# Hybrid Hyena and attention backbone: the front of layer 0 ordered by channel halves, its filter butterflies on VectorE

## The chip, the cores and the metric

The kernel runs on one core of a Trainium2 chip. The metric is the device time in microseconds (us) of one execution; the time before is the median of three runs. TensorE, VectorE, ScalarE and GpSimd are named PE, DVE, ACT and POOL in the profile; PEld is TensorE's loading of weights, SP the engine that only issues DMAs.

## The reference

A trunk of two layers over 1024 tokens of width 1024, with 256 context tokens, all in float32. Layer 0 joins two mixers. The Hyena mixer projects 3 x 512 channels (v, x1, x2), puts a short convolution of three taps over each, and then twice convolves over the whole sequence with a filter that a small network makes:

```python
def hyena_mix(proj, conv_w, conv_b, w1, b1, freq, w2, b2, w3, d_skip):
    proj = dwconv3(proj, conv_w, conv_b)
    v, x1, x2 = jnp.split(proj, 3, axis=-1)
    filt = hyena_filters(L, w1, b1, freq, w2, b2, w3)
    z = v
    for o, gate in enumerate((x1, x2)):
        z = gate * fftconv_bidir(z, filt[:, o], d_skip[o])
    return z
```

The other is differential attention of four heads, whose keys and values come from the tokens and from the context, with rotary positions on q and k. Both go through one output projection. Behind them stand a convolutional feed-forward network, layer 1 (a spatial gating unit) and a second feed-forward network; none of these is touched.

## The kernel before

The change lies in `layer0_front`, the first quarter of the kernel. Matrices are split into a high and a low part (`split`, L144): the high part is a cast on ScalarE, the low part a subtraction on VectorE or GpSimd, and a product is three matmuls (`mm3`, L156). The strings at the top, such as `F_PART` and `F_H`, say with a letter for each operation whether VectorE (V) or GpSimd (G) does it.

The front first makes the normalised input: `hhi[k]`, `hlo[k]` (eight tiles of 128 channels by 1024 tokens, L409 to 417; `F_H` chooses the engine of the low parts) and `hch`, `hcl` for the context. Then two generators run:

- `main` (L785) is the projections, TensorE's work: `proj_v` (values of tokens and context), `proj_kc` (keys of the context), `proj_hyena` (12 units of 128 channels: for each half of the 512 Hyena channels the kinds v, x1, x2, each in two units; a unit is 96 matmuls and two shifted multiply-adds on VectorE, L672 to 674), and `proj_qk` (8 units; each is rotated with a table `tab`, L756, and stored).
- `side` (L789) is the long convolutions. `filters` (L505) makes the spectra of all filters and stores them to `Hd` in DRAM: for each of two orders it loads and splits w3 (1024 columns), and for each half of the channels and each side `sd` it makes one set: products with the window (`z`), and `dft_part` (L470), a transform whose first step is matmuls and whose second is 13 small sums, the butterflies, which `F_PART` places. Then `conv_chain` (L614) for each half: transform of `z`, product with the stored spectrum, inverse transform, gate, twice over. It stops where `z`, x1 or x2 of its half is not yet projected.

`eager` (L161) traces the two: the side as far as it goes, then one step of main, and so on. So all eight sets of filters are traced first, then proj_v, proj_kc and the first three Hyena units, then the first part of the convolution chain, and so on. The traced order is not yet the engines' order. A planner at compile time gives each engine its list: among the instructions whose operands and buffers it reckons to be ready, the one traced earlier goes first, and what stands under `first()` (L185) counts as traced 4000 instructions earlier. The lists are fixed; at run time each engine and each DMA queue works in its own order and waits on semaphores.

Buffers come from pools and are given in the planner's order. `f8` (L306, 7 tiles of 128x2048 float32) holds `hch`, `hcl`, the raw and split w3, `z` of each half and the operands of all transforms, and the table `tab`; attention loads its first head into the same seven. `t4` (4 tiles of 128x1024) serves the projections and the last step of the chain. `h8` (2 tiles) holds the window, the spectra and the gates. In `proj_qk` the two parts of the rotated result go to `t4`, or to `h8` when the side has been traced to its end (L766). Weights come by SP's queue into two buffers, and w3 (L512), `dskip` (L526) and the table by the same queue; stores and `h8` loads go by ScalarE's queue.

```python
            def main():
                for gen in (proj_v(), proj_kc(), proj_hyena(), proj_qk()):
                    yield from gen

            def side():
                yield from filters()
                ld(tbi, ap["dfti"])
                for half in range(2):
                    yield from conv_chain(half)
                done.add("side")
```

Of the kernel before, what the change touches and what calls it, by code (L numbers as in the profile page):

```python
# [92 lines left out]
def tile_kernel(ctx: ExitStack, tc: tile.TileContext, ap: dict, out: bass.AP, stop=None):  # L93
# [6 lines left out]
    def nm(s):  # L100
        uid[0] += 1
        return f"{s}_{uid[0]}"
# [185 lines left out]
    def layer0_front(fp):  # L288
        with ExitStack() as es:
# [10 lines left out]
            def ps4():  # L300
                return ps2("pf").rearrange("p (r n) -> p r n", r=4)
# [4 lines left out]
            def f8(dt=F32):  # L306
                return fp.tile([P, 2, 4, CH], dt, tag="f8", name=nm("f8"))

            def f8z(dt=F32):
                return f8(dt).rearrange("p a b n -> p (a b) n")  # L310

            def h8(src, shape):
                t = h8pool.tile([P, 2048], F32, tag="h8", name=nm("h8"))
                st(t, src)
                return t.rearrange("p (a b c) -> p a b c", a=shape[0], b=shape[1])
# [186 lines left out]
                stt(V, X[:, 1, 2:4], u[:, 1, 0:2], -RT2, t[:, 1, 0:2], MUL, ADD)  # L502
                return X

            def filters():  # L505
                h2r = h2s.rearrange("p (s r) -> p r s", r=8)
                for o in range(2):
                    raw = f8()
                    w3, w3s = raw.rearrange("p a b n -> p a (b n)")[:64, 0], None
                    w3 = raw[:64, 0].rearrange("p (a b) n -> p a (b n)", a=2)  # L510
                    w3s = raw[:64, 1].rearrange("p (a b) n -> p a (b n)", a=2)
# [3 lines left out]
                    ws = f8(F32R)  # L515
                    w3h = ws[:, 0].rearrange("p (a b) n -> p a (b n)", a=2)
                    w3l = ws[:, 1].rearrange("p (a b) n -> p a (b n)", a=2)
                    A.copy(out=w3h[0:64], in_=w3s)
                    A.copy(out=w3h[64:128], in_=w3s)
                    sub(V, w3l[0:64], w3s, w3h[0:64])  # L520
                    sub(V, w3l[64:128], w3s, w3h[0:64])
                    for half in range(2):
                        win = h8(ap["window"][half], (1, 8))[:, 0]
                        cs = slice(half * CH, (half + 1) * CH)
                        dsk = tp.tile([P, CH], F32, tag="dsk", name=nm("dsk"), bufs=1)
                        ld(dsk[0:1], ap["dskip"][o : o + 1, cs])  # L526
                        for sd in range(2):
                            z = f8z()
                            for g in range(2):
                                ps = ps4()  # L530
                                for r in range(4):
                                    mm(ps[:, r], h2r[:, g * 4 + r], w3h[:, sd, cs], True, False)
                                    mm(ps[:, r], h2r[:, g * 4 + r], w3l[:, sd, cs], False, True)
                                gs = slice(g * 4, g * 4 + 4)
                                mul(V, z[:, gs], ps, win[:, gs])
                            if sd == 0:

                                p0 = ps2("pf")
                                mm(p0[:, :CH], h2r[:, 0], w3h[:, 1, cs], True, False)
                                mm(p0[:, :CH], h2r[:, 0], w3l[:, 1, cs], False, True)  # L540
                                f0 = tp.tile([P, CH], F32, tag="f0", name=nm("f0"), bufs=1)
                                mul(V, f0[0:1], p0[0:1, :CH], win[0:1, 0])
                                add(V, f0[0:1], f0[0:1], z[0:1, 0])
                                V.tensor_scalar(out=f0[0:1], in0=f0[0:1], scalar1=0.5, scalar2=None, op0=MUL)
                                stt(V, z[0:1, 0], dsk[0:1], 1.0 / S, f0[0:1], MUL, ADD)
                            yield
                            X = yield from dft_part(z, sd, 2 * o + half)
                            for par in range(2):
                                st(Hd[o, half, par][:, sd * 1024 : (sd + 1) * 1024],
                                   X[:, par].rearrange("p a b -> p (a b)"))  # L550
                            yield


            zs, done = {}, set()
# [163 lines left out]
                        st(Kd[h, i][:, S:], r32(t[:, i * CTX : (i + 1) * CTX]))  # L718
                    yield

            def proj_hyena():
                z = {}

                def post(half, kind, j, a):
                    if kind == 2:
                        st(x2d[2 * half + j], a)
                        done.add((1, half, j))
                        return
                    ps = to_time(a)
                    if kind == 0:  # L730
                        if j == 0:
                            z[half] = f8z()
                        with first():
                            A.copy(out=z[half][:, :, j * P : (j + 1) * P], in_=ps)
                        if j == 1:
                            zs[half] = z[half]
                    else:
                        t = t4()
                        with first():
                            A.copy(out=t, in_=ps.rearrange("p r c -> p (r c)"))  # L740
                        st(x1d[half][:, :, j * P : (j + 1) * P], t.rearrange("p (r c) -> p r c", r=8))
                        done.add((0, half, j))

                pend = None
                for half in range(2):
                    for kind in range(3):
                        for j in range(2):
                            a = conv_mtile(4 * kind + 2 * half + j)
                            if pend:
                                post(*pend)  # L750
                            pend = (half, kind, j, a)
                            yield
                post(*pend)

            def proj_qk():
# [39 lines left out]

# [1078 lines left out]
```

## Time and profile before

| | |
|---|---|
| time, median of 3 runs | 2723.33 us (2721.12 to 2727.28) |
| the profiled execution: its time | 2731.36 us |
| the profiled execution: its span | 2729.3 us |
| busy, share of the span | PE 91%, DVE 66%, ACT 44%, POOL 40% |
| mean granted clock of TensorE | 0.959 |
| instructions | 30518 |

The span is the time from the first to the last instruction of the profiled execution; the time of that execution is 2 us longer. The shares are means over stages with different limits, so a change in one stage has to be read from that stage.

### The profile page before, as it was taken

To read this page: it belongs to the slowest core of one execution; us is meant where nothing else is said; L and a number is where in the kernel's file an instruction comes from. 1 tells how busy PE (TensorE), PEld (TensorE's weight loads), DVE (VectorE), ACT (ScalarE), POOL (GpSimd) and SP (SyncE) were. 2 spreads that over 40 slices of the span, in tenths; PEclk is the share of its full clock that TensorE was granted. 3 is DMA by queue.
4 is the path that set the end of the run, shared out by engine and by line. 5 is a ranking of instruction groups with operands and counts; after the bars stand their busy time and mean duration, and the time that the engine had idled before them with its cause. 6 is when DMAs were issued, how large, how long until landed. Compare 5 with 4: busy or idle time off the path is not lost. (4 is left out here: it accounts for less than half of the span.)

```text
span 2729.3 us, 30518 instructions
## 1 busy us (share of the span) xinstructions
PE 2482.1 (91%) x11192; PEld 1978.6 (72%) x11192; DVE 1795.3 (66%) x2119; ACT 1205.1 (44%) x1871; POOL 1086.2 (40%) x819
## 2 busy tenths in 40 slices
PE   6799878697888899999999899999999999999897
PEld 1798767576777667777777777778877777777676
DVE  4677788878896485666666966532366665567854
ACT  2312211026665256555554355313356566555342
POOL 1323111103443352423334777413343433438775
PEclk8899998898999899999999999999999999999998
DMA  7224222257732446988787634111436777769422
GB/s 284 66 101 166 85 101 85 70 186 231 201 100 66 162 116 152 246 218 228 201 224 254 227 115 147 39 45 48 156 84 148 179 167 171 180 155 320 143 81 101
DMA packets 166854, 412.75 MB, mean 151 GB/s; under 512 B 16011, under 2 KB 28815, under 8 KB 164528
## 3 DMA queue, kind: packets, MB, share of 16 engines
q1 hardware_dynamic: 86352, 248.76, 28.7%
q0 software_dynamic: 34848, 63.45, 13.6%
q10 hardware_dynamic: 45504, 98.58, 9.8%
q8 instruction: 88, 1.44, 0.2%
q14 instruction: 62, 0.51, 0.1%
HBM read 261.31 MB, written 85.98 MB: 127 GB/s over the span
## 5 line engine op out<-in xcount | busy, mean ns | idle before, releaser
L154 PE MATMUL b<-u,u 128*128 128x512 f32 (+1 forms) x5624 | 1328.5, 395 | 66.3 <-POOL u L132 25.6
L154 PEld LDWEIGHTS b<-u,u 128*128 128x128 f32 x5624 | 1060.2, 191 | 332.9 <-POOL u L132 36.5
L132 DVE TENSOR_TENSOR u<-u,u 128x512 fp32r<-128x512 f32 (+2 forms) x470 | 468.5, 1024 | 334.8 <-ACT u L1141 173.9
L132 POOL TENSOR_TENSOR u<-u,u 128x512 fp32r<-128x512 f32 (+1 forms) x338 | 505.4, 1516 | 295.5 <-ACT u L1141 176.6
L1152 POOL DMA_DIRECT2D u<-u x242 | 211.3, 920 | 490.3 <-ACT u L1151 378.4
L1141 ACT CAST u<-u 128x512 fp32r<-128x512 f32 x462 | 261.6, 616 | 231.4 <-DVE u L132 96.8
L154 PE MATMUL b<-x,u 128*128 128x512 f32 x1224 | 296.8, 397 | 1.8 <-ACT u L1342 1.1
L128 DVE SCALAR_TENSOR_TENSOR u<-u,cols,u 128x1023 f32<-128x1023 f32 x176 | 232.6, 1328 | 95.2 <-ACT u L1588 87.1
L154 PEld LDWEIGHTS b<-x,u 128*128 128x128 f32 x1224 | 229.4, 188 | 62.9 <-issue 3.4
L1150 ACT CAST u<-u 128x512 fp32r<-128x512 f32 x242 | 146.2, 614 | 120.8 <-DVE u L132 94.7
L132 POOL TENSOR_TENSOR wlo<-wraw,whi 128x1024 fp32r<-128x1024 f32 x24 | 68.9, 2874 | 314.2 <-ACT whi L147 311.1
L1151 ACT ACTIVATE u<-u 128x512 fp32r<-128x512 f32 x242 | 149.4, 628 | 71.8 <-POOL u L132 62.7
L132 DVE TENSOR_TENSOR u<-u,b 128x512 f32<-128x512 f32 (+1 forms) x132 | 112.1, 860 | 66.0 <-PE b L154 65.2
L132 DVE TENSOR_TENSOR f<-f 128x256 f32<-128x256 f32 (+3 forms) x232 | 148.4, 699 | 1.0
L154 PE MATMUL pj<-hh,whi 128*128 128x512 f32 x320 | 130.7, 408 | 19.8 <-ACT t L740 8.3
L1588 ACT ACTIVATE u<-u,cols 128x1024 f32<-128x1024 f32 x88 | 109.3, 1242 | 87.5 <-DVE u L132 85.0
L128 DVE SCALAR_TENSOR_TENSOR x<-b,mods,x 128x512 f32<-128x512 f32 (+1 forms) x104 | 88.7, 906 | 66.4 <-PE b L154 66.4
L154 PE MATMUL pj<-hl,whi 128*128 128x512 f32 x320 | 128.0, 400 | 0.0
L154 PE MATMUL pj<-hh,wlo 128*128 128x512 f32 x320 | 127.9, 400 | 0.0
L132 POOL TENSOR_TENSOR p<-p,p 128x1280 f32<-128x1280 f32 x27 | 79.6, 2948 | 121.2 <-ACT p L885 103.3
L874 ACT ACTIVATE p<-s,nx 128x1280 f32<-128x1280 f32 x64 | 84.9, 1328 | 44.7 <-DVE nx L870 41.8
L147 ACT CAST whi<-wraw 128x1024 fp32r<-128x1024 f32 x28 | 29.2, 1047 | 164.2 <-PE pj L154 145.8
(225 smaller groups left out, 3115.8 us busy)
## 6 DMA issues: line engine op xcount, KB each, us to landing
u<-u POOLq DMA_DIRECT2D x242, 256.0 KB, 4.6
u<-wup SPq DMA_DIRECT2D x88, 512.0 KB, 4.7
Td<-u ACTq DMA_DIRECT2D x66, 512.0 KB, 5.6
u<-Td SPq DMA_DIRECT2D x56, 512.0 KB, 4.4
wraw<-modw SPq DMA_DIRECT2D x48, 512.0 KB, 5.3
u<-wdown SPq DMA_DIRECT2D x40, 512.0 KB, 5.8
wraw<-modw0b SPq DMA_DIRECT2D x32, 512.0 KB, 3.9
xs<-x ACTq DMA_DIRECT2D x48, 256.0 KB, 2.1
```

The costliest lines, as they stand in the source:

```text
L128: eng.scalar_tensor_tensor(out=o, in0=a, scalar=sc, in1=b, op0=op0, op1=op1)
L132: eng.tensor_tensor(out=o, in0=a, in1=b, op=op)
L147: A.copy(out=hi, in_=x)
L154: T.matmul(o, l, r, start=st and not onto, stop=sp, skip_group_check=onto)
L874: A.activation(q.p[m], q.s, AF.Exp, bias=q.nx, accum_out=q.l[:, m : m + 1])
L1141: A.copy(out=t[:, H0], in_=x)
L1150: A.copy(out=t[:, H0], in_=x)
L1151: A.activation(t[:, H1], t[:, H0].bitcast(F32), AF.Copy, scale=-1.0)
L1152: G.dma_start(out=t[:, H1], in_=x, accum_op=ADD)
L1588: A.activation(a, c, AF.Identity, bias=col(f"fb{l}", f), scale=col(f"fw{l}1", f))
```

## The change

Filters and projections are ordered by channel halves. `filters` takes a half and makes the four sets of that half only (both orders, both sides); its w3 load and split take 256 of 512 columns of each side and happen four times instead of twice. `proj_hyena` takes a half too. `main` runs Hyena's first half, the values, Hyena's second half, the context keys, then queries and keys. `side` runs filters and convolution of half 0, then filters and convolution of half 1. All letters of `F_PART` and `F_H` become V.

```diff
-F_PART = ("VGGGVGGVVVVVG", "VGGVVGGVVVVVV", "VGGGVGGVVVVVG", "VGGVVGGVVVVVV", "VGGGVGGVVVVVG", "VGGVVGGVVVVVV", "VGGGVGGVVVVVG", "VGGVVGGVVVVVV")
+F_PART = ("V" * 13,) * 8
...
-F_H, F_X, F_SQ = "VGVVGVVG", "VVVVVVVV", ("V", "V", "V", "V", "V", "V", "V")
+F_H, F_X, F_SQ = "VVVVVVVV", "VVVVVVVV", ("V", "V", "V", "V", "V", "V", "V")
...
-            def filters():
+            def filters(half):
                 h2r = h2s.rearrange("p (s r) -> p r s", r=8)
+                cs = slice(half * CH, (half + 1) * CH)
                 for o in range(2):
...
+                    raw, ws = f8(), f8(F32R)
+                    w3, w3s = (raw[:64, i, 0:2] for i in range(2))
-                    ld(w3, ap["hy_w3"][:, o])
+                    ld(w3, ap["hy_w3"][:, o, :, cs])
                     add(V, w3s[:, 0], w3[:, 0], w3[:, 1])
                     sub(V, w3s[:, 1], w3[:, 0], w3[:, 1])
...
-                    for half in range(2):
-                        win = h8(ap["window"][half], (1, 8))[:, 0]
-                        cs = slice(half * CH, (half + 1) * CH)
+                    win = h8(ap["window"][half], (1, 8))[:, 0]
...
-            def proj_hyena():
+            def proj_hyena(half):
                 z = {}
...
-                for half in range(2):
-                    for kind in range(3):
-                        for j in range(2):
-                            a = conv_mtile(4 * kind + 2 * half + j)
+                for kind in range(3):
+                    for j in range(2):
+                        a = conv_mtile(4 * kind + 2 * half + j)
...
             def main():
-                for gen in (proj_v(), proj_kc(), proj_hyena(), proj_qk()):
+                for gen in (proj_hyena(0), proj_v(), proj_hyena(1), proj_kc(), proj_qk()):
                     yield from gen
 
             def side():
-                yield from filters()
                 ld(tbi, ap["dfti"])
                 for half in range(2):
+                    yield from filters(half)
                     yield from conv_chain(half)
                 done.add("side")
```

## Rows read from the trace of the kernel before

**Rows 1.** The page's second part: TensorE's busy tenths in 40 slices.
```profile
PE   6799878697888899999999899999999999999897
```

**Rows 2.** Timeline of TensorE: start us, duration us, instruction, [idle before <-releaser].
```profile
546.70 9.46 PE L154 MATMUL pf<-tbi,f 128*128 128x128 f32 x64 [25.11 <-DVE f L132]
...
619.04 2.43 PE L154 MATMUL s<-f,f 128*128 128x512 f32 x6 [2.53 <-ACT t L773]
```

**Rows 3.** By stretch: busy us (xcount) of PE, PEld, DVE, ACT, POOL; clock; DMA.
```profile
76.00:111.00 35.00, 25.26 (x145) 23.80 (x145) 23.26 (x17) 15.80 (x20) 15.64 (x5) 0.70 0.16 50
111.00:191.00 80.00, 78.56 (x483) 74.43 (x482) 56.63 (x77) 14.97 (x16) 21.22 (x22) 1.00 0.33 114
191.00:270.00 79.00, 74.96 (x394) 66.78 (x394) 59.67 (x79) 17.27 (x21) 30.71 (x26) 1.00 0.42 142
270.00:296.00 26.00, 21.87 (x98) 18.08 (x97) 6.30 (x6) 7.12 (x7) 4.70 (x2) 0.93 0.19 61
296.00:430.00 134.00, 105.49 (x483) 88.39 (x482) 116.31 (x145) 20.68 (x20) 20.33 (x6) 0.90 0.27 94
430.00:565.00 135.00, 102.15 (x471) 85.03 (x471) 119.07 (x149) 17.52 (x17) 13.93 (x4) 0.89 0.29 91
```

**Rows 4.** Timeline of all engines around 270 to 299 us.
```profile
269.28 0.68 DVE L128 SCALAR_TENSOR_TENSOR f<-f,f 128x512 f32<-128x512 f32 x1
...
275.36 1.00 ACT L734 COPY f<-pj 128x1024 f32<-128x1024 f32 x1
...
291.11 1.00 ACT L734 COPY f<-pj 128x1024 f32<-128x1024 f32 x1
...
295.99 2.48 DVE L132 TENSOR_TENSOR f<-pf,f 128x1024 f32<-128x1024 f32 x2 [2.15 <-PE pf L154]
```

**Rows 5.** Timeline of ScalarE and its DMA queue over the front.
```profile
107.82 0.40 ACTq L704 DMA_DIRECT2D Vd<-t  x1
...
236.01 0.33 ACTq L718 DMA_DIRECT2D Kd<-t  x1
...
410.39 1.93 ACT L734 COPY f<-pj 128x1024 f32<-128x1024 f32 x2 [11.86 <-DVE f L132]
...
570.48 1.02 ACT L773 ACTIVATE t<-pj 128x1024 f32<-128x1024 f32 x1 [11.20 <-DMA yd<-t]
...
617.97 1.02 ACT L773 ACTIVATE t<-pj 128x1024 f32<-128x1024 f32 x1 [1.66 <-DVE h L132]
```

**Rows 6.** Waits of SP's queue, 0 to 640 us: in total, times, longest.
```profile
SPq L526 <- DVE f L128: 58.3, 3, 38.0
...
SPq L758 <- DVE f L132: 14.6, 1, 14.6
```

**Rows 7.** VectorE by shape, 296 to 565 us: busy us, mean ns.
```profile
L132 DVE TENSOR_TENSOR f<-f 128x256 f32<-128x256 f32 x92 | 38.5, 486 | 0.1
L128 DVE SCALAR_TENSOR_TENSOR t<-pj,cols,t 128x1023 f32<-128x1023 f32 x18 | 22.9, 1274 | 2.2 <-ACT t L672 2.2
```

**Rows 8.** Groups by shape in the filter stage, 111 to 270 us.
```profile
L132 DVE TENSOR_TENSOR f<-f 128x256 f32<-128x256 f32 x56 | 34.1, 646 | 0.8
...
L132 POOL TENSOR_TENSOR f<-f 128x256 f32<-128x256 f32 x40 | 32.0, 808 | 98.5 <-DVE f L132 92.8 <-PE pf L154 4.7 <-DMA Kd<-t 0.2
```

**Rows 9.** Timeline of VectorE in the filter stage.
```profile
111.64 1.22 DVE L132 TENSOR_TENSOR f<-pf,h 128x1024 f32<-128x1024 f32 x1 [8.89 <-PE pf L154]
...
184.07 0.68 DVE L132 TENSOR_TENSOR f<-f 64x512 f32<-64x512 f32 x1
...
190.69 1.23 DVE L132 TENSOR_TENSOR f<-pf,h 128x1024 f32<-128x1024 f32 x1 [2.37 <-PE pf L154]
```

**Rows 10.** DMA issues, 100 to 270 us: KB each, median us to landing.
```profile
Hd<-f ACTq DMA_DIRECT2D x16, 512.0 KB, 3.2
```

**Rows 11.** Timeline of GpSimd while h is split.
```profile
91.47 4.08 POOL L132 TENSOR_TENSOR hl<-t,hh 128x1024 fp32r<-128x1024 f32 x1 [3.61 <-ACT hh L147]
```

**Rows 12.** VectorE's groups by shape, 70 to 640 us.
```profile
L132 DVE TENSOR_TENSOR t<-t,f 128x1024 f32<-128x1024 f32 x16 | 20.8, 1340 | 0.1
```

More of the change, by code (lines that the diff above doesn't have):

```diff
@@ L503, in dft_part @@
                 return X
[L505 removed]
+            def filters(half):
                 h2r = h2s.rearrange("p (s r) -> p r s", r=8)
+                cs = slice(half * CH, (half + 1) * CH)
                 for o in range(2):
[L508 to L511, printed above, removed]
[L512 removed]
+                    raw, ws = f8(), f8(F32R)
+                    w3, w3s = (raw[:64, i, 0:2] for i in range(2))
+                    ld(w3, ap["hy_w3"][:, o, :, cs])
                     add(V, w3s[:, 0], w3[:, 0], w3[:, 1])
                     sub(V, w3s[:, 1], w3[:, 0], w3[:, 1])
[L515 to L517 removed]
+                    w3h, w3l = (ws[:, i, 0:2] for i in range(2))
                     A.copy(out=w3h[0:64], in_=w3s)
@@ L521, in filters @@
                     sub(V, w3l[64:128], w3s, w3h[0:64])
-                    for half in range(2):
-                        win = h8(ap["window"][half], (1, 8))[:, 0]
-                        cs = slice(half * CH, (half + 1) * CH)
[L525 to L551, printed above, removed]
@@ new lines, in filters @@
+                    win = h8(ap["window"][half], (1, 8))[:, 0]
+                    dsk = tp.tile([P, CH], F32, tag="dsk", name=nm("dsk"), bufs=1)
+                    ld(dsk[0:1], ap["dskip"][o : o + 1, cs])
+                    for sd in range(2):
+                        z = f8z()
+                        for g in range(2):
+                            ps = ps4()
+                            for r in range(4):
+                                mm(ps[:, r], h2r[:, g * 4 + r], w3h[:, sd], True, False)
+                                mm(ps[:, r], h2r[:, g * 4 + r], w3l[:, sd], False, True)
+                            gs = slice(g * 4, g * 4 + 4)
+                            mul(V, z[:, gs], ps, win[:, gs])
+                        if sd == 0:
+                            p0 = ps2("pf")
+                            mm(p0[:, :CH], h2r[:, 0], w3h[:, 1], True, False)
+                            mm(p0[:, :CH], h2r[:, 0], w3l[:, 1], False, True)
+                            f0 = tp.tile([P, CH], F32, tag="f0", name=nm("f0"), bufs=1)
+                            mul(V, f0[0:1], p0[0:1, :CH], win[0:1, 0])
+                            add(V, f0[0:1], f0[0:1], z[0:1, 0])
+                            V.tensor_scalar(out=f0[0:1], in0=f0[0:1], scalar1=0.5, scalar2=None, op0=MUL)
+                            stt(V, z[0:1, 0], dsk[0:1], 1.0 / S, f0[0:1], MUL, ADD)
+                        yield
+                        X = yield from dft_part(z, sd, 2 * o + half)
+                        for par in range(2):
+                            st(Hd[o, half, par][:, sd * 1024 : (sd + 1) * 1024],
+                               X[:, par].rearrange("p a b -> p (a b)"))
+                        yield
@@ L744, in proj_hyena @@
                 pend = None
-                for half in range(2):
-                    for kind in range(3):
-                        for j in range(2):
-                            a = conv_mtile(4 * kind + 2 * half + j)
[L749 to L752, printed above, removed]
+                for kind in range(3):
+                    for j in range(2):
+                        a = conv_mtile(4 * kind + 2 * half + j)
+                        if pend:
+                            post(*pend)
+                        pend = (half, kind, j, a)
+                        yield
                 post(*pend)
```

## The prediction

> **What bounds the kernel now.** I read the page's slices first, then TensorE's idle places, a table of engine time by stretch over the front, the timelines around single places, and groups by shape. Behind the front TensorE is busy in nine tenths of most slices, and the front lasts to about 619 us, when the first attention scores start [rows 1, 2]; nothing behind it is touched, so what the front gains or loses should arrive at the end one for one.
>
> The front divides at places that rows show. From 76 to 111 the normalised input is made. From 111 to 270 the eight filter sets run (two filter orders, two halves, two sides), about 19.8 us each; TensorE is nearly full here (78.6 of 80, 75.0 of 79), filled by the value and context-key projections, while VectorE works 56.6 + 59.7 = 116.3 of 159 us [rows 3]. From 270 to 296 VectorE has almost nothing, 6.3 of 26 us: the filters are done at 269.96, but the first forward transform needs the first half's projected z, whose two copies end at 276.4 and 292.1, and its first sum starts at 295.99 [rows 3, 4]. From 296 to 430 and from 430 to 565 the two convolution chains run with VectorE at 116.3 of 134 and 119.1 of 135 us: they are one serial chain of VectorE work. TensorE then lacks 28.5 and 32.9 us [rows 3]. Two causes can be seen: before 410 the copies of the second half's z wait 11.86 us for VectorE to give up a tile [rows 5], and before 546.7 TensorE stands 25.11 us behind VectorE's inverse transform [rows 2]. The load of the rope table depends on nothing but a free `f8` tile, and SP still waits 14.6 us for VectorE before it [rows 6]; the rotations of q and k start after it. Behind the chain TensorE has query/key units left, one each (617.97 - 570.48) / 5 = 9.5 us [rows 5]. So what sets the start of attention is VectorE's chain from 111 to 565, plus five query/key units.
>
> **The change part by part**, as differences on that chain.
>
> *The gap at 270.* z of half 0 is now the first thing projected. In the old order two units were 15.75 us apart [rows 4]; from about 92 us both are done near 130, long before four filter sets end. What stays is the way from a ready z to the first sum, 295.99 - 292.11 = 3.9 us. 26.0 - 3.9: -22 us. I choose this in full, since z has about 60 us to spare.
>
> *Short convolution off the chain.* Of 24 such VectorE instructions 18 lie between 296 and 565, 1.274 us each [rows 7]. Half of the 24 now fall into the first filter stage, where VectorE idles: six fewer on the busy chain, -8. Bounds -8 and 0.
>
> *Butterflies.* F_PART turns 40 GpSimd instructions (808 ns) into VectorE ones [rows 8]. At the 486 ns of the same shape in the convolution stage [rows 7] that is +19.4. Against it: in the filter stage the 56 that VectorE has already take 646 ns [rows 8]; at 486 they give back 56 x 0.16 = 9.0. VectorE is also idle 159 - 116.3 = 43 us in the eight sets, 5.3 per set [rows 3], and the five even-half operations of a set (2.4 us) need only the first pair of PSUM reads, so they can lie in such a wait. Bounds +19 (none hidden, nothing given back) and -9 (all hidden); I take +2, nearer to hidden, since the wait is longer than the work. That VectorE slows beside GpSimd is what these two means show. The Trainium skill (SBUF — State Buffer, section on the two physically separate sides) says that the two share a port pair as an exclusive lock, for which a VectorE instruction with two SBUF inputs competes, and the loser blocks for the whole instruction. By it up to 40 x 0.81 = 32 us of blocking could go, and this term would be -13 where I have +2; 160 ns more per instruction is much less than that.
>
> *Weights of the filters.* w3 is prepared four times at half size instead of twice. One cost the way from 184.07 to the next product at 190.69, 6.6 us [rows 9]; I estimate 4.5 at half width, since part of it is cast and waiting. 4 x 4.5 - 2 x 6.6 = +5. Bounds 0 and +13 (two more at full price).
>
> *Tiles.* The `f8` pool has seven. The context halves `hch`, `hcl` are read by proj_v and proj_kc, which were over at 236 [rows 5]; proj_kc is now behind both Hyena halves, so two tiles stay held far longer, and z of half 0 holds a third through the first four sets. With the filter weights that leaves three for z, a, b, t, X. It can still run (b is free before X is needed) but the next set's two products, 1.22 us each [rows 9], no longer overlap with the last sums: 3 boundaries x 2.4 = +7. Bounds 0 and +70: per set 2.4 plus X's two stores in turn, 3.2 us each to land [rows 10], 8.8 x 8.
>
> *Filling.* The second half's filters are traced behind the first chain and may run in its waits: 134 - 116.3 = 17.7 us [rows 3]. Bounds -17.7 and 0; -5, for want of tiles.
>
> *Splits of h.* Three low halves go from GpSimd, whose last took 4.08 us [rows 11], to VectorE, where 128x1024 operands take 1.22 [rows 9]: the last about 3 us earlier, -3; bounds -4 and 0.
>
> *SP's queue.* Four w3 loads instead of two and four dskip loads now stand among the Hyena weights. SP stood up to 38 us on a dskip wait [rows 6]; behind it are projection weights. Two units of weights in hand cover 19 us of TensorE, and VectorE's chain doesn't wait for them: 0, bound +19. GpSimd only loses work; it issues no loads here.
>
> *The tail.* Unit 0 of the query/key projection took its two output halves from the four `t4` tiles, since the side was not yet traced to its end; with proj_kc between, all eight use `h8`, and one more unit can stand done before the chain ends. -9.5; bounds -47.5 (all five) and +9.5.
>
> Sum: -22 - 8 + 2 + 5 + 7 - 5 - 3 - 9.5 = -33.5 us. The profiled execution has a span of 2729.3 and a time of 2731.4, 8 us above the median 2723.3; that offset is not touched, so I forecast 2723.3 - 33.5 = 2690, with 2672 to 2708 as this case's own range.
>
> **The rivals.**
> - *Tiles starve the filters; slower.* The place is the first writer of X or of the next z, the price up to 8.8 us per set. At full price +70 stands for +7: -33.5 + 63, 2753. It decides from (7 + 33.5) / 8 = 5.1 us per set. For it: the rope load, which needs only a free tile, found none until the last transform [rows 6], so the pool is always full. Against it: the old filters also ran beside `hch`, `hcl`, with only one tile more. Chance 0.17.
> - *VectorE is the bound; nothing gained.* Butterflies at +19.4, no hiding of short convolutions (0), no filling (0): -33.5 + 17.4 + 8 + 5 = -3, 2720. Against it: VectorE is idle 43 of 159 us in the filter stage [rows 3]. The Trainium skill (Perfetto Trace Analysis, Optimizing Scalar/DVE Operations) advises handing work from a saturated VectorE to others, even GpSimd; by that rule this change goes the wrong way in the convolution stage, but the moved work lies where the trace shows idle time. Chance 0.11.
> - *The rope table gets a tile early; more gained.* Four more units move before the chain's end, 4 x 9.5 = -38, but bring a shuffle, two products, a sum and a split of VectorE each, by the products' 1.34 us [rows 12] an estimated 6.5, +26: 2678. Against it: the table has the last claim on tiles. Chance 0.12. All of TensorE's idle time from 76 to 565, 9.7 + 1.4 + 4.0 + 4.1 + 28.5 + 32.9 = 80.6 us [rows 3], gives the floor, 2643.
> - *The order does not change on the engines.* They follow a compiled order, not the text: a tile of proj_v was stored at 107.82, before the first product of the filters at 111.64, which are traced ahead of it [rows 5, 9]. If the planner fills as before, only butterflies and weights change: +7 or less, 2723 to 2730. Chance 0.06.
>
> **How the numbers follow.** The forecast has 0.54. The range runs from just above the floor, 2645, to 2735, which leaves out most of the starving case (about 0.14) and a little below. A change of 0.2% (5.4 us) is about what a measurement of this kernel can tell from none. Faster: 0.54 + 0.12 + 0.04 of the VectorE case + 0.02 of a mild starving = 0.72. Same: 0.05 + 0.04 + 0.01 = 0.10. Slower: 0.02 + 0.02 + 0.14 = 0.18.
>
> **What would show it.** Right: no idle stretch of VectorE between the fourth filter set and the first forward sum; filter sets of 18 to 21 us; first scores near 585 instead of 619; four or fewer query/key units after the last inverse transform; no GpSimd work on 128x256 tiles. Wrong: VectorE waiting between sets with X's stores or tile releases as the cause (sets of 25 us or more), z of half 1 waiting tens of us for a tile with TensorE empty, or a longer row of query/key units after the chain.

## The result, and the profile after

The changed kernel takes 2686.73 us (median of 4 runs, 2685.09 to 2689.07) against 2725.28 for the kernel before (4 runs): 38.5 us less, ratio 0.9861 with a 95% interval of 0.9844 to 0.9878. The profiled spans are 2729.3 and 2686.4 us. The forecast was 2690, so the gain was 5 us larger than forecast (38.5 for 33.5). The sum was right; several of its terms were not, and their errors cancelled.

The front is shorter. Its end is taken here at the first score matmul, 615.21 before and 577.88 after: 37.3 us. The row at 619.04 [rows 2], which the prediction took for the first scores, is the second row of them. The code behind the front is not touched, but the time from the first scores to the end of the span isn't quite the same from one profiled execution to the next: 2114.1 us before, 2108.5 after, and between 2104.4 and 2115.7 in the fourteen kernels of this document. So a few us of a time need not come from the front, and 5.6 of the 42.9 us between the two spans don't. The last stand of TensorE before the inverse transform fell from 25.11 to 14.88 us. VectorE's last product of the chain and TensorE's first scores before, and the same places after:

```profile
564.34 1.20 DVE L132 TENSOR_TENSOR t<-pf,t 128x1024 f32<-128x1024 f32 x1
615.21 1.30 PE L154 MATMUL s<-f,f 128*128 128x512 f32 x6
```

```profile
513.19 3.17 PE L154 MATMUL pf<-tbi,f 128*128 128x128 f32 x13 [14.88 <-DVE f L132]
...
524.36 1.22 DVE L132 TENSOR_TENSOR t<-pf,t 128x1024 f32<-128x1024 f32 x1
...
577.88 2.73 PE L154 MATMUL s<-f,f 128*128 128x512 f32 x12
583.34 1.84 PE L154 MATMUL s<-f,f 128*128 128x512 f32 x6 [2.72 <-ACT p L869]
```

The front now has other stretches: 68 to 96 ends the preparation of the input, 96 to 173 is the first half's four filter sets, 173 to 301 its convolution chain, 301 to 380 the second half's filters, 387 to 524 its chain, and from 524 on TensorE has only queries and keys. Busy time by stretch, after, to be held against [rows 3] (columns as there):

```profile
96.00:173.00 77.00, 67.22 (x291) 57.32 (x291) 63.76 (x102) 17.78 (x19) 7.10 (x3) 0.96 0.28 98
173.00:301.00 128.00, 117.08 (x741) 108.10 (x741) 112.31 (x142) 19.17 (x20) 16.75 (x5) 0.96 0.33 114
301.00:380.00 79.00, 77.83 (x365) 67.66 (x366) 63.05 (x100) 16.31 (x18) 9.65 (x4) 1.00 0.32 112
380.00:387.00 7.00, 5.69 (x30) 4.92 (x29) 2.56 (x2) 4.06 (x4) 2.35 (x1) 1.00 0.19 77
387.00:524.00 137.00, 111.83 (x548) 95.70 (x547) 123.12 (x150) 22.73 (x25) 35.96 (x7) 0.91 0.32 104
524.00:579.00 55.00, 55.00 (x245) 45.53 (x243) 40.88 (x40) 15.19 (x15) 4.81 (x2) 1.00 0.70 231
```

The old stand of 26 us [rows 4] is gone: VectorE's last operation of the fourth filter set ends at 172.96, and the first forward sum starts at 173.10. A small new one is at 380, where the second half's z is late. VectorE's timeline after, at both places and at the start of the filters:

```profile
83.41 4.62 DVE L132 TENSOR_TENSOR hl<-t,hh 128x1024 fp32r<-128x1024 f32 x4
87.95 0.74 DVE L132 TENSOR_TENSOR f<-f 64x256 f32<-64x256 f32 x2
89.39 5.03 DVE L132 TENSOR_TENSOR f<-f,f 64x512 fp32r<-64x512 f32 x2 [0.69 <-ACT f L516]
96.47 1.23 DVE L132 TENSOR_TENSOR f<-pf,h 128x1024 f32<-128x1024 f32 x1 [2.06 <-PE pf L154]
...
171.67 1.29 DVE L128 SCALAR_TENSOR_TENSOR f<-f,f 128x512 f32<-128x512 f32 x2
173.10 2.49 DVE L132 TENSOR_TENSOR f<-pf,f 128x1024 f32<-128x1024 f32 x2
...
378.51 1.29 DVE L128 SCALAR_TENSOR_TENSOR f<-f,f 128x512 f32<-128x512 f32 x2
382.36 2.60 DVE L128 SCALAR_TENSOR_TENSOR t<-pj,cols,t 128x1023 f32<-128x1023 f32 x2 [2.55 <-ACT t L668]
387.11 2.48 DVE L132 TENSOR_TENSOR f<-pf,f 128x1024 f32<-128x1024 f32 x2 [2.15 <-PE pf L154]
```

The first product of the filters starts at 96.47 where it was 111.64 [rows 9]: 15 us earlier, five times what I had for it. And the butterflies: VectorE by shape, in the first and in the second filter stage after, to be held against the 56 at 646 ns of [rows 8]:

```profile
L132 DVE TENSOR_TENSOR f<-f 128x256 f32<-128x256 f32 x48 | 17.4, 414 | 0.1
L132 DVE TENSOR_TENSOR f<-f 128x256 f32<-128x256 f32 x48 | 17.8, 419 | 0.2
```

VectorE does 96 of them in 35.2 us; before it did 56 in 34.1. The 40 that came over from GpSimd cost it 1 us of busy time.

One thing doesn't show as a stand of VectorE. The first half's z is ready early: TensorE has transposed its two units at 117.84 and 147.62. But ScalarE copies them out of the projections' two PSUM tiles (`pj`) only at 166.59, right behind the last matmuls of the fourth filter set, and from 147.62 to 167.66 TensorE has no projection matmul. It is busy 13.99 of these 20.1 us, with the filters. TensorE and ScalarE, after:

```profile
146.46 1.16 PE L678 MATMUL pj<-ident,t 128*128 128x128 f32 x8
164.94 1.56 PE L154 MATMUL pf<-f,tbf 128*128 128x256 f32 x6 [0.89 <-ACT f L479]
166.59 1.93 ACT L730 COPY f<-pj 128x1024 f32<-128x1024 f32 x2 [1.71 <-PE pf L154]
167.66 0.50 PE L154 MATMUL pj<-hh,whi 128*128 128x512 f32 x1 [1.16 <-ACT f L730]
```

By the code the copies write an `f8` tile, and the matmuls named as their releaser read one. So I read this as z waiting for a tile that the filters hold, while it holds both PSUM tiles of the projections. No run gave z a tile of its own.

At the end nothing moved forward: the last product ends VectorE's chain at 525.6 (before 565.5), and five query/key units still follow, (578.09 - 526.06) / 5 = 10.4 us each, as five did in [rows 5]. ScalarE's timeline after, first and last of the q copies behind the chain:

```profile
526.06 1.03 ACT L768 ACTIVATE t<-pj 128x1024 f32<-128x1024 f32 x1 [3.30 <-DMA yd<-t]
...
578.09 1.03 ACT L768 ACTIVATE t<-pj 128x1024 f32<-128x1024 f32 x1 [3.77 <-PE pj L154]
```

### The profile page after: what moved, and what is told of

Read it like the earlier page. It is cut to its first block, busy times and chain, and to the rows that moved or that the text cites. A ratio compares the mean times of both kernels' runs of the same rounds, so it can differ in the third digit from the quotient of the medians.

```text
span 2686.4 us, 30496 instructions
## 1 busy us (share of the span) xinstructions
PE 2475.8 (92%) x11192; PEld 1974.0 (73%) x11192; DVE 1804.1 (67%) x2170; ACT 1206.3 (45%) x1875; POOL 1058.9 (39%) x776
## 5 line engine op out<-in xcount | busy, mean ns | idle before, releaser
L132 POOL TENSOR_TENSOR wlo<-wraw,whi 128x1024 fp32r<-128x1024 f32 x24 | 81.7, 3414 | 395.8 <-ACT whi L147 395.8
L865 DVE TENSOR_REDUCE nx<-s 128x1 f32<-128x1280 f32 x64 | 94.6, 1480 | 4.8 <-PE s L154 4.3
```

The costliest lines, as they stand in the source:

```text
L132: eng.tensor_tensor(out=o, in0=a, in1=b, op=op)
L865: V.reduce_max(out=q.nx, in_=q.s, axis=AX.X, negate=True)
```

## The experiments

Times are medians, each against the kernel before on the same chip. "Chain end" is the end of VectorE's last product of the second chain, "scores" the first score matmul (565.5 and 615.2 before, 525.6 and 577.9 after).

| kernel | us | to before | ratio (95%) | chain end | scores |
|---|---|---|---|---|---|
| changed | 2686.73 | -38.5 | 0.9861 (0.9844 to 0.9878) | 525.6 | 577.9 |
| letters alone | 2717.77 | -7.7 | 0.9978 (0.9966 to 0.9989) | 555.9 | 605.9 |
| letters and small w3 | 2722.33 | -4.8 | 0.9987 (0.9976 to 0.9997) | 554.7 | 604.8 |
| order alone | 2704.86 | -20.6 | 0.9930 (0.9918 to 0.9942) | 541.6 | 594.0 |
| changed, old butterflies | 2699.54 | -26.0 | 0.9906 (0.9891 to 0.9920) | 534.6 | 586.9 |
| changed, filters not halved | 2730.18 | +4.7 | 1.0020 (1.0010 to 1.0030) | 564.6 | 616.9 |
| changed, old projections | 2752.71 | +27.4 | 1.0103 (1.0085 to 1.0121) | 584.5 | 634.5 |
| changed, both Hyena halves first | 2724.53 | -0.8 | 0.9999 (0.9988 to 1.0010) | 504.1 | 614.1 |
| changed, values cut in two | 2708.43 | -16.9 | 0.9937 (0.9921 to 0.9953) | 533.1 | 600.8 |
| changed, five t4 | 2695.35 | -30.0 | 0.9887 (0.9871 to 0.9904) | 549.8 | 585.8 |
| changed, first w3 early | 2699.21 | -27.9 | 0.9894 (0.9878 to 0.9909) | 538.6 | 591.7 |
| changed, tile for w3 | 2696.50 | -26.6 | 0.9910 (0.9890 to 0.9929) | 535.2 | 587.5 |
| changed, tile for later w3 | 2704.19 | -22.8 | 0.9913 (0.9897 to 0.9929) | 542.2 | 594.5 |

**Letters or order.** Three runs cut the change into its letters and its order (the order goes with w3 at half size).

```diff
# letters alone: the kernel before, and
+F_PART = ("V" * 13,) * 8
+F_H = "VVVVVVVV"
```

> The kernel before with the two engine letters alone: the butterflies of the filters and all splits of h on VectorE, order and weights as before. My theory (the order made the gain, the letters next to none): VectorE still stands about 26 us between the last filter set and the first forward sum, because the last z copy near 292 us is set by the order of the projections, and a filter stage that ends earlier only makes that stand longer; -3 us against before, between -8 and +2. Rival (the letters did it: GpSimd out of the filter stage lets VectorE run faster and the whole chain moves): 25 to 38 us less than before, the chip's first forward sum 15 us or more earlier.

```diff
# order alone: the changed kernel, and
+F_PART = ("VGGGVGGVVVVVG", "VGGVVGGVVVVVV", ...) 
+F_H = "VGVVGVVG"
```

> The new order and the weights at half size, but the old engine letters: 40 butterflies and three splits of h stay on GpSimd. My theory: the stand before the first forward sum is gone (under 5 us), and the time is 25 to 33 us below before. What the letters add is at most the later start of the filters (their first product 3 to 8 us later than in the changed kernel) and 128x256 VectorE operations of about 640 ns in place of 415 in the filter stages. Rival (the letters did it): within 10 us of before.

```diff
# changed, old butterflies: the changed kernel, and
+F_PART = ("VGGGVGGVVVVVG", "VGGVVGGVVVVVV", ...)
```

> The changed kernel with the old letters for the butterflies alone: 40 operations on 128x256 back on GpSimd, splits of h stay on VectorE. If GpSimd and VectorE hold each other up (theory), the 128x256 operations of VectorE in the filter stages go from 415 to about 640 ns, VectorE's busy time there is the same to within 3 us, and the filter stages are 3 to 8 us longer each: 3 to 15 us slower than the changed kernel. Rival 1 (VectorE is the bound and GpSimd's share is a real help): 5 to 15 us faster than the changed kernel. Rival 2 (VectorE's waits hide either): within 3 us.

Order alone gives -20.6, the splits of h 5.3 more (order alone to old butterflies), the butterflies 12.6 more (old butterflies to changed). At the first scores these are 21.2, 7.0 and 9.1 us. My theory of "next to none" for the letters fell, though the -7.7 in the old order still lie inside its range of -8 to +2. There the filters' first product is at 103.47 for 111.64, the first forward sum at 287.06 for 295.99, and the stand before it is 20.4 us. VectorE's timeline in the run with the letters alone:

```profile
265.38 1.29 DVE L128 SCALAR_TENSOR_TENSOR f<-f,f 128x512 f32<-128x512 f32 x2
...
287.06 2.48 DVE L132 TENSOR_TENSOR f<-pf,f 128x1024 f32<-128x1024 f32 x2 [2.15 <-PE pf L154]
```

The stand did not grow, as I had expected, because the filter stage did not shrink: 163.2 us (103.47 to 266.67) for 158.3, with TensorE busy 78.70 of 80 us from 111 to 191 and 73.26 of 76 from 191 to 267. From the first product to the first forward sum it is 183.6 us for 184.4. So in the old order the earlier start went through, and the butterflies gave next to nothing. In the run with the order alone the stand is gone, as the theory had it (182.11 follows 181.98), but the gain fell 4 us short of its 25. The parts aren't additive: -7.7 and -20.6 make -38.5 together.

What the butterflies cost on GpSimd is to be seen in the second filter stage of the run with the old letters. Groups by shape of that run, 301 to 392 us:

```profile
L132 DVE TENSOR_TENSOR f<-f 128x256 f32<-128x256 f32 x28 | 16.6, 627 | 0.4
L132 POOL TENSOR_TENSOR f<-f 128x256 f32<-128x256 f32 x20 | 16.1, 813 | 68.8 <-DVE f L132 66.7 <-PE pf L154 1.7
```

28 operations of VectorE take 16.6 us beside GpSimd's 20, where 48 alone take 17.8. Single rows of the same run say how: three operations of VectorE, of a shape that takes 0.42 us each in the changed kernel, take 4.26 us while GpSimd works.

```profile
375.81 2.40 POOL L132 TENSOR_TENSOR f<-f 128x256 f32<-128x256 f32 x3 [3.58 <-DVE f L132]
378.18 2.56 POOL L132 TENSOR_TENSOR wlo<-wraw,whi 128x1024 fp32r<-128x1024 f32 x1
...
376.76 4.26 DVE L132 TENSOR_TENSOR f<-f 128x256 f32<-128x256 f32 x3
```

The other rivals fell: neither is VectorE the bound (the run would be faster) nor do waits hide it. The 9.0 us by which its chain ends later (534.6 for 525.6) divide into 1.8 at the start, 0.6 to the second filters, 3.2 in that stage (81.5 for 78.3), 4.3 in a longer wait for the second z, and -0.9 in the last chain. Of the 1.8 at the start, 1.7 stood already in the input, ahead of any butterfly (GpSimd's first weight split at 70.58 for 68.89). The first filter stage grew by only 1.1 us (77.6 for 76.5), less than the 3 to 8 that I expected of each. So the holding up is shown directly for some 4 us; why the second z came later was not looked for.

**Half the order.** Two runs keep one of the two orderings each.

```diff
# filters not halved: the changed kernel, and
             def side():
                 ld(tbi, ap["dfti"])
                 for half in range(2):
                     yield from filters(half)
+                for half in range(2):
                     yield from conv_chain(half)
```

> The changed kernel with all eight filter sets ahead of both convolution chains, so that only the projections are ordered by halves, and w3 is still loaded four times at half size. Theory A (the gap at 270 us is closed because z of half 0 is projected first; putting the filters half by half is worth nothing by itself): within 6 us of the changed kernel, no stand of VectorE before the first forward sum, nor before the second half's, since its z is then long done; the 7 us stand at 380 us goes too. Theory B (the half-by-half filters are needed, because z of both halves and the halves of the context take tiles from eight sets in a row): 10 to 30 us slower than the changed kernel, filter sets of 21 us or more.

```diff
# old projections: the changed kernel, and
-                for gen in (proj_hyena(0), proj_v(), proj_hyena(1), proj_kc(), proj_qk()):
+                for gen in (proj_v(), proj_kc(), proj_hyena(0), proj_hyena(1), proj_qk()):
```

> The changed kernel with the projections in the old order (values and context keys, then Hyena half 0, half 1, queries and keys), while the filters stay half by half. Theory (the two orders only work together): four filter sets are done near 175 us, z of half 0 is not there before 240 us or later, VectorE stands 60 us or more, and the time is 30 to 80 us above the changed kernel, so above before too. Rival (the half-by-half filters are what gains): within 10 us of the changed kernel.

Both halves of the order, alone, are worse than the kernel before. With projections by halves and all filters first, there is no wait at the first forward transform; it is at the second. VectorE's timeline of that run:

```profile
394.65 2.60 DVE L128 SCALAR_TENSOR_TENSOR t<-pj,cols,t 128x1023 f32<-128x1023 f32 x2 [18.83 <-ACT t L668]
405.53 2.60 DVE L128 SCALAR_TENSOR_TENSOR t<-pj,cols,t 128x1023 f32<-128x1023 f32 x2 [8.28 <-ACT t L668]
419.66 2.60 DVE L128 SCALAR_TENSOR_TENSOR t<-pj,cols,t 128x1023 f32<-128x1023 f32 x2 [11.53 <-ACT t L668]
426.10 2.48 DVE L132 TENSOR_TENSOR f<-pf,f 128x1024 f32<-128x1024 f32 x2 [3.83 <-PE pf L154]
```

From 375.8 to 426.1 VectorE has 7.8 us of work, while TensorE is at the second half's projections; between 376 and 427 it is busy 45.17 of 51 us. Theory A missed: I had the second z "long done". What made it late, as I read the rows, stands earlier in the run. The first z is transposed by 148.85, but copied only at 243.07, now behind the eighth set instead of the fourth, and in between TensorE has no projection matmul: from 148.9 to 244 it is busy 61.98 of 95.1 us. TensorE and ScalarE of that run:

```profile
147.69 1.16 PE L678 MATMUL pj<-ident,t 128*128 128x128 f32 x8
243.07 1.93 ACT L730 COPY f<-pj 128x1024 f32<-128x1024 f32 x2 [1.71 <-PE pf L154]
244.14 0.50 PE L154 MATMUL pj<-hh,whi 128*128 128x512 f32 x1 [1.16 <-ACT f L730]
```

Theory B gave the right side, but not the size or the place: the run is 43 us slower than the changed kernel, beyond its 30, and its eight filter sets take 151.5 us (97.9 to 249.4) against 76.5 + 78.3. A lack of tiles doesn't lengthen the sets; by the rows above it holds up z, and with z the projections. With the filters by halves and the old projections the wait is at the first transform again, from 174.8 to 244.1, 69 us, as that theory had it. By these traces the order gains in three ways: the projections by halves put the first z ahead of the first chain, the filters by halves let z leave the projections' PSUM tiles after four sets instead of eight, and 78 us of filters of the second half lie between the two chains, in which TensorE makes the second z. Each ordering alone moves the wait.

**How early is best.** If a late z is the trouble, an earlier one should help.

```diff
# both Hyena halves first
+                for gen in (proj_hyena(0), proj_hyena(1), proj_v(), proj_kc(), proj_qk()):
# values cut in two (proj_v does one half of its columns)
+                for gen in (proj_hyena(0), proj_v(0), proj_hyena(1), proj_v(1), proj_kc(), proj_qk()):
```

> The changed kernel with both halves of Hyena projected first, then values, context keys, queries and keys. Theory (VectorE's chain and TensorE's supply of other work must fit stage by stage; z of half 1 holds a tile from early on, and values and keys are left for the end): the 7 us stand at 380 us is gone, but TensorE stands idle in the second filter stage and has values, context keys and all eight query/key units behind the last inverse transform: 10 to 45 us slower than the changed kernel. Rival (the earlier z is, the better): 3 to 8 us faster than the changed kernel.

> The changed kernel with the value projection cut in two: half of it between the two Hyena halves as before, half behind the second. It puts z of half 1 about 15 us of TensorE work earlier. Theory A (the 7 us stand of VectorE at 380 us lies on the path): the stand is gone and the time is 3 to 8 us below the changed kernel. Theory B (TensorE's total is what binds, the work is only moved behind the chain): no change or up to 15 us slower, with more units behind the last inverse transform.

With both halves first, VectorE's chain ends 21.5 us earlier than in the changed kernel (504.1), and the scores start 36 us later (614.1). Busy time by stretch of that run:

```profile
235.00:305.00 70.00, 44.88 (x218) 38.68 (x216) 60.20 (x76) 7.55 (x8) 5.61 (x2) 0.80 0.21 71
305.00:376.00 71.00, 50.00 (x190) 41.97 (x190) 52.24 (x94) 10.76 (x13) 0.00 (x0) 0.86 0.24 87
```

TensorE lacks 25 and 21 us there. From 281.28 to 372.38 it has no projection matmul: the second half's z, transposed by 281.28, is copied only at 371.31, behind the eighth set. TensorE and ScalarE of that run:

```profile
279.34 1.94 PE L678 MATMUL pj<-ident,t 128*128 128x128 f32 x8 [7.08 <-DVE t L128]
371.31 1.93 ACT L730 COPY f<-pj 128x1024 f32<-128x1024 f32 x2 [1.71 <-PE pf L154]
372.38 0.50 PE L154 MATMUL pj<-hh,whi 128*128 128x512 f32 x1 [1.16 <-ACT f L730]
```

Behind the chain it then has 110 us of values, keys and queries to do. With the values cut in two the wait at 380 is gone as well, but TensorE lacks 26 us between 240 and 400 (no projection from 354.50 to 390.48, in the same way) and has 68 us left behind the chain. So theory B held in its direction (the second run is 22 us slower than the changed kernel, above its 15), and the first run's theory with 38 us: removing the 7 us at 380 in these ways cost more than they are worth. TensorE's last query/key unit stands ahead of the first scores in each of these runs, so its idle time counts wherever it falls. From 68 us to the first scores it is busy 453.9 us in the changed kernel and 459.5 with both halves first, and idle 56.0 and 86.6.

**The tail, and tiles.** Five t4 tiles let one or two more query/key units be done ahead.

```diff
-F8, T4 = 7, 4
+F8, T4 = 7, 5
-                w1 = tp.tile([P, 64], F32, tag="fw1", ...); w2 = ...
+                fw = t4()
+                w1, w2 = fw[:, 0:64], fw[:, 64:128]
```

> The changed kernel with five t4 tiles in place of four (two small weight tiles of the filter network moved into a t4 tile to make room). Theory (the tail stayed at five query/key units because the two prefetched x2d blocks of the last transform hold two of the four t4 tiles, so that query/key units can't be started ahead): one or two more units are done before the last inverse transform, TensorE's stand of 15 us before 513 us is filled, first scores 8 to 14 us earlier, 2673 to 2679 us. Rival (the units need VectorE too, and only push the chain back): within 4 us of the changed kernel.

The units did move: 36.0 us lie between chain end and scores instead of 52.3. But the chain ends 24.2 us later. Of this 8.4 stood already at the second half's first product (309.9 for 301.5); from there to the scores it takes 275.9 us, in the changed kernel 276.4. The theory fell. In that stretch the rival held: a unit done ahead brings a shuffle, products and splits of VectorE into a chain in which VectorE is busy 123.12 of 137 us, and gained nothing. In time the run is 8.6 us above the changed kernel, more than the rival's 4, by what it lost before that stretch.

Two runs took the raw w3 off the f8 pool, all four loads or the last three (w1 and w2 are in a t4 tile there too):

```diff
-                    raw, ws = f8(), f8(F32R)
+                    raw = tp.tile([P, 2, 2, CH], F32, tag="w3", ..., bufs=1)   # second run: only if o or half
+                    ws = f8(F32R)
```

> The changed kernel with a tile of its own for the raw w3 (two small weight tiles of the filter network moved into a t4 tile to make room), so that its load no longer waits for one of the seven f8 tiles and the products have one more. Theory A (tiles cost the filter stages something, the +7 of the sum): the second load of w3 is issued before 110 us instead of at 127, the sets behind a w3 preparation shrink from 22 and 25 us towards the 16 us of the others, and the time is 4 to 12 us below the changed kernel. Theory B (the sets are set by the order that the planner gives VectorE, not by tiles): the load comes early but the sets stay, within 4 us of the changed kernel or above it.

> The run with a tile of its own for w3, but the first of the four preparations keeps its f8 tile, as in the changed kernel, so that the first weights of the projections are not behind the load of w3. Theory A (the start cost that run its gain: a 128x1024 operation of GpSimd took 14.65 us there beside VectorE's splits of h, and TensorE stood 11.4 us for it): first product back at 96 to 98 us, the sets behind a w3 preparation stay at 20 to 21 us, first scores 3 to 9 us before the changed kernel's, 2678 to 2684 us. Theory B (the second chain waits for z of half 1, which TensorE sets): first product back, but VectorE's stand before the second chain grows to 10 us or more, within 4 us of the changed kernel.

In the first of them the second load was issued at 95.03 instead of 127.15, and the two sets that end with a w3 preparation shrank from 21.8 and 25.1 us to 19.7 and 20.6 (19.8 and 20.6 in the second). So tiles do cost something here, 2 and 4.5 us, as theory A said. Both runs are slower than the changed kernel all the same, mostly because they start late: first product at 104.6 and 108.6. GpSimd's second split of the first weights now falls beside VectorE's splits of h. GpSimd and TensorE of the first of the two runs:

```profile
74.80 14.65 POOL L132 TENSOR_TENSOR wlo<-wraw,whi 128x1024 fp32r<-128x1024 f32 x1 [3.26 <-ACT whi L147]
```

```profile
89.51 0.80 PE L154 MATMUL pj<-hh,wlo 128*128 128x512 f32 x1 [11.38 <-POOL wlo L132]
```

An operation that took 2.34 us at 69.20 in that run takes 14.65, and TensorE waits for it. My cure for the second run (the first load back in its old tile) cured nothing: GpSimd's two splits took 20.1 us together there, the first load of w3 was issued only at 91.07, VectorE stood 9.48 us for it, and theory A missed on the start and on the time.

**The weights w3.**

```diff
# first w3 early: the changed kernel, with set 0's w3 prepared ahead of the context's square
+            early[0, 0] = w3_prep(0, 0)
             sq = f8z()
# letters and small w3: "letters alone", with load, sums, casts and splits of w3
# moved into the loop over halves, 256 columns each
+                    for half in range(2):
+                        ld(w3, ap["hy_w3"][:, o, :, cs])
```

> The changed kernel with the first preparation of w3 (its load, sum, difference, two casts and two splits) put ahead of the context's normalisation, where VectorE stands 13 us at 49 us. Theory A (what the filters start earlier arrives at the end one for one): first filter product near 88 to 90 us instead of 96.5, and 5 to 8 us below the changed kernel. Theory B (TensorE's supply of z of half 1 sets the second chain): the filters start 7 us earlier, but VectorE's stand before the second chain, 7 us at 380 us, grows by as much, and the time is within 4 us of the changed kernel.

> The kernel before with both engine letters and w3 prepared four times at half size, everything else in the old order. Theory (the smaller first w3 is what put the filters' first product from 103.5 to 96.5 us, and the later ones are hidden): first product 95 to 97 us, stand of some 25 us before the first forward sum as before, 2 to 8 us below the run with the letters alone (2710 to 2716). Rival, as the sum of the prediction had it (four preparations at half size cost 5 us more than two at full size): 2720 to 2726.

Preparing w3 early didn't put the first product earlier (95.9 for 96.5): VectorE waited 8.64 us for the load at 59.8, and the context's and part of h's work fell behind it. So neither theory was tried; the third set then began at 146.0 instead of 138.1, and the run is 11 us slower. The small w3 in the old order does start the filters sooner (97.1 for 103.5, of which 2.9 stood already in the input, 69.21 for 72.07), but the later preparations cost: from the second set to the third and the sixth to the seventh, where one was added, are 30.2 and 31.8 us where the run with the letters alone has 22.0 and 22.4; from the fourth to the fifth, where both have one, 24.3 and 25.8. The stage ends 7.1 us later (273.73 for 266.67), and the stand before the first forward sum (285.22 for 287.06) takes it up. The time lies in the rival's range (2722.33), but it doesn't settle the sum's +5: 4.8 and 7.7 us below before have overlapping intervals, and the first scores come 1.2 us earlier than with the letters alone, or 1.7 later without the 2.9 of the input.

## Why the prediction was right

In sum, and in the mechanism of the largest term: the wait at 270 closed, and the first scores came 37.3 us earlier where the sum had 33.5. The rest of the size is luck, by errors that cancel. Term by term, in the profiled executions, from the first filter product to the chain's end (the terms found make 39.9 at the chain's end, 37.3 at the first scores):

| step of the sum | forecast | found |
|---|---|---|
| start of the filters (splits of h) | -3 | -15.2 |
| filter sets (butterflies +2, weights +5, tiles +7) | +14 | -3.5 (158.3 to 76.5 + 78.3) |
| gap | -22 | -18.6 (26.0 to 0.1 + 7.3) |
| chains (short convolution -8, filling -5) | -13 | -2.6 (134.0 + 135.5 to 128.4 + 138.5) |
| tail | -9.5 | +2.6 (49.7 to 52.3) |
| sum | -33.5 | -37.3 |

- *Gap.* Right in what closes it, and nearly in size; not foreseen are the 7.3 us that came back at 380. And z did not have the 60 us to spare that the term was chosen by: its copies end at 168.52, 4.6 us before the first sum, and the 20 us without projections that its wait brought stand in no term.
- *Start.* Mis-sized. I priced the splits of h by the last one alone. VectorE's last split ends at 88.0 where GpSimd's ended at 95.55 [rows 11], and letters alone, with the input ready as before (GpSimd's first weight split at 72.07 and 72.05), start the filters 8.2 us earlier. Another 3.2 us are the input, whose first weight split starts at 68.89; that moment lies between 66.99 and 72.23 in runs whose edits don't touch what precedes it, so I count it to no part (each was profiled once, so kernel and run can't be told apart). The remaining 3.8 are order and w3, and the small w3 in the old order gives 3.5 of the kind (103.47 to 97.06, less the 2.9 of the input): I had put all four preparations into one term and missed that the first stands alone at the head of the chain.
- *Butterflies.* The wrong sign: +2, "nearer to hidden". The run with the old letters puts it at -12.6 in time and -9.0 at the chain's end, of which 1.7 are input and 4.3 the second z. The term had let the 56 operations give back 9.0 us; they fell from 646 to 416 ns, which is 12.9. The Trainium skill's rule that I weighed against it (SBUF — State Buffer, section on the two physically separate sides: the two engines share a port pair as an exclusive lock, and the loser blocks) gave -13. The trace agrees with its kind, by the single rows above, in which VectorE's three operations end with GpSimd's; it doesn't agree with the 32 us of blocking behind that -13, of which 12.9 came back. The other section of the Trainium skill that the prediction named (Perfetto Trace Analysis, Optimizing Scalar/DVE Operations) says that handing work of a saturated VectorE to others may make sense, but adds that between VectorE and GpSimd, which share a port, it might not help. The prediction left that out. The measurement here agrees with it: the 40 operations that came back to VectorE cost it 1 us of busy time.
- *Weights.* Not settled. In the old order the filter stage is 13.5 us longer with the small w3 (97.06 to 273.73 for 163.2), at the term's upper bound, and the stand behind it hides that; in the changed kernel the sets with a preparation are 22 and 25 us beside 16 to 21.
- *Tiles.* +7 was of the right size, 2 + 4.5 by the runs with a tile for w3, and far from the starving rival; but the place was wrong. The term counted three boundaries between sets (there are six). What the runs show is a wait before w3 (SP's longest is 20.3 us) and, as I read it, z held in the projections' PSUM tiles.
- *Chains.* Short convolutions did move: VectorE has six of these instructions in each of the two filter stages (with the stand at 380) and the two chains, so twelve instead of 18 in the chains [rows 7]. The first chain fell by 5.6 us. The second grew by 3.0, with 4 us more of VectorE's busy time than [rows 3] have there; what of it was not looked for.
- *Tail.* Failed: still five units. That the prefetched x2d blocks hold two of the four t4 tiles is argued only. But the run with five t4 shows that the term was ill-posed: I gave a unit done ahead 9.5 us of TensorE and nothing of VectorE's time in the chain, though I had priced that in a rival.

So the forecast of the time rested on errors of -12 and -17.5 against +3.4, +10.4 and +12.1; that they leave 4 us is luck. Of the marks that I had set, three held (no wait before the first transform, scores some 34 us earlier, with 37 measured, no GpSimd work on these tiles), the sets are 16 to 25 us instead of 18 to 21, and the four or fewer units did not come. A mark of being wrong, z waiting tens of us for a tile, came with the first z: 19 us, from 147.62 to 166.59, TensorE not empty but without projections.

What stays open: five small alterations of the changed kernel (values cut in two, five t4, early w3, the two tiles for w3) all end 8 to 22 us above it. In the last four, 6 to 9 us of it stand already at the third set (143.9 to 147.3 for 138.1). Whether the gains seen later (sets of 20 us, no wait at 380) can be had with the changed kernel's start wasn't settled, nor what a tile for z alone would give.

## What to carry to other kernels

Ask of an order not where a wait closes, but where it goes: sum up the work of the feeding engine (TensorE here) ahead of each due point, and the chain's engine at each of them, before you price a gap as gone. Ask too where an early result will lie until it is used: with no tile free it can hold the PSUM that the feeding engine needs next, as z seems to have done here. A part that gives nothing in the old order can count in the new one, as the butterflies did here, so price letters in the order in which they will run. And before giving an idle GpSimd part of VectorE's SBUF work, read the same shape's mean with and without GpSimd beside it.

## What the runs showed of the hardware

The holding up goes both ways and isn't shared fairly. VectorE's 128x256 operations take 414 to 419 ns in the filter stages of the changed kernel (456 in the run with the letters alone) and 598 to 646 where GpSimd does 20 or 40 of them; beside VectorE's splits of h, from 74.79 to 87.25, one GpSimd operation went from 2.34 to 14.65 us. And in the changed kernel GpSimd's split of the context does it to VectorE, at the head of the chain: the two 64x512 splits of w3 took 5.03 us from 89.39, where the run with the early w3 has 1.38 for the same two. GpSimd's timeline, after:

```profile
88.28 4.89 POOL L132 TENSOR_TENSOR f<-f,f 128x2048 fp32r<-128x2048 f32 x1 [14.29 <-ACT f L147]
```

That these 3.7 us would be gained by another place or engine for the context's split wasn't tried.
